# A running NaN-skipping row maximum: the last 36 tiles divided anew, single-buffer waits for the key passes, shared write-back semaphores from tile 42 on

## The chip, the cores and the metric

The kernel runs on one core of a Trainium2 chip. The metric is the time of one execution on the device in microseconds (us); lower is better. The profile was taken in one such execution.

## The reference

```python
def reference(x: np.ndarray, axis: int) -> np.ndarray:   # x: 32 x 2048 x 2048 f32, a tenth of it NaN; axis -1
    return np.nanmax(x, axis=axis).astype(np.float32)
```

Each of the 65,536 rows of 2048 numbers gives its largest number that is not a NaN. 536.87 MB are read and 0.26 MB written.

## The kernel before

Every one of the 128 partitions has 512 rows of x to itself. Work is counted in **quarters**: a quarter is 512 of a row's 2048 elements on all partitions, 256 KB in all, and there are 2048 of them. They are cut into 69 **tiles**, numbered from 0: tile 0 has 4 quarters, tiles 1 to 35 have 32 (8 rows), tiles 36 to 68 have 28 (7 rows). Three tiles fit into the buffer `full`.

A tile goes through four stages, one engine or queue each:

- **Load.** SP issues the DMA of a tile, in one or several pieces. The load of tile n waits for the last reduce of tile n-3, which frees the buffer (`free`, passed as `before`).
- **Key pass** (the ACTIVATE with `Prelu`, `e_key`). ScalarE (ACT) reads the upper 16 bits of each float and makes of it a number in which a NaN falls to the bottom. Below tile 38 (`PLAIN`) the keys are written over the upper half of the data itself; from there on into one of three **key buffers** (`kts`) of 12 quarters. One of these is a tile of its own, which the profile calls kt; the other two lie in a part of `full` that is free by then, so the profile calls them xt. When a chunk doesn't fit behind the last one, the next key buffer is taken, and the key pass has to wait until what was in it has been written back (`kfree`, `freed`).
- **Write-back** (`write`). The keys are turned back and put into the upper halves of the floats, with NaNs gone. GpSimd (POOL) does most, ACT some, and in tiles 1 to 33 VectorE (DVE) five quarters a tile.
- **Reduce** (`maxima`). DVE takes the maximum of a stretch of rows once its write-backs are there.

Which quarters go where is written out by hand in `TILES`, one entry a tile: the load pieces, then the chunks, each with its key passes and its write-backs, then the reduces, all in quarters. A plain number among the write-backs is POOL's. A pair (n, w) is ACT's and is issued after w more key passes; with w = -1 it is DVE's. Each engine runs its instructions in the order in which they are issued.

Two devices stand beside that table. `joints` looks for a reduce that needs exactly one last write-back of POOL and one of ACT; the two then raise one shared semaphore, `pairN_i`, in place of each engine's own, and whoever waits for one of the two waits for both. And `EARLY` is a list of tiles: in these, the last key pass of a tile, if it takes a new key buffer, waits for that buffer and for the one after it as well.

The lines that do this:

```python
kold = freed(key, (key + 1) % NKEYS) if number in EARLY and at + c == end else freed(key)
```

```python
pairs[number] = joints(keys, backs, reds)
```

Of the kernel before, what the change touches and what calls it, by code (L numbers as in the profile page):

```python
# [16 lines left out]
TILES = (  # L17
    [([4], [([4], [4])], [4])]
    + [([32], [([12], [(5, -1), 7]), ([12], [12]), ([8], [8])], [12, 12, 8])] * 32
# [14 lines left out]
    + [([28], [([7], [7]), ([9], [9]), ([12], [12])], [16, 12])] * 3  # L34
    + [([28], [([8], [1, (2, 2), 5]), ([6, 3], [9]), ([11], [11])], [16, 12])]
    + [([28], [([6], [6]), ([10], [10]), ([12], [12])], [16, 12])]
    + [([28], [([8], [8]), ([9], [9]), ([11], [11])], [8, 8, 12])] * 2
# [6 lines left out]
    + [([16, 12], [([8], [8]), ([8], [8]), ([12], [7, (5, 0)])], [8, 8, 12])] * 2  # L44
# [7 lines left out]
)  # L52


# [19 lines left out]
WIDE = 8  # L74
FULL = 36
PLAIN = 38

NARROW = (0, 17 * D // 2, 31 * D // 2)
BUFS = 3
# [7 lines left out]

LANES = 14

EARLY = (0, 1, 2, 3, 4, 5, 6, 7, 8, 9, 10, 11, 12, 13, 14, 15, 16, 17, 18, 19, 20, 21, 22, 23, 24, 25, 26, 27, 28, 29, 30, 31, 32, 33, 34, 35, 36, 37, 38, 39, 40, 41, 42, 43, 44, 45, 46, 47, 48, 49, 50, 51, 52, 53, 54, 55, 56, 63)  # L90

# [11 lines left out]
def joints(keys, backs, reds):  # L103


    parts = []
    pieces = []
    at = end = step = 0
    for n, wait in backs:
        end += n  # L110
        while at < end:
            at += keys[step]
            step += 1
        if wait is None or wait >= 0:
            parts.append((end - n, end, wait is not None, step + (wait or 0), len(pieces)))
        pieces.append(n)
    needs = []
    done = 0
    for n in map(abs, reds):
        over = [i for i, p in enumerate(parts) if p[0] < done + n and p[1] > done]  # L120
        done += n
        pools = [i for i in over if not parts[i][2]]
        acts = sorted((i for i in over if parts[i][2]), key=lambda i: parts[i][3])
        if pools and acts and parts[pools[-1]][3] > parts[acts[-1]][3]:
            acts = []
        needs.append(pools[-1:] + acts[-1:])
    pairs = {}
    for need in needs:
        if len(need) == 2 and all(sum(i in n for n in needs) == 1 for i in need):
            both = tuple(parts[i][4] for i in need)  # L130
            for i in both:
                pairs[i] = both
    return pairs
# [62 lines left out]
def kernel(  # L196
# [91 lines left out]
    with tc.tile_critical() as section:  # L288
# [72 lines left out]
        pairs = {}  # L361
        half = {}

        def write(number, a, b, k, kp, e, i, back):
# [27 lines left out]
            for a, b, k, back, when in both:  # L392
                if number >= PLAIN:
                    kfree[k][back] = max(kfree[k].get(back, ((0, 0), None)), (when, e))
                clean[number].append((a, b, e, back))

        def freed(*ks):

            uses = [(back, then, e) for k in ks for back, ((_, then), e) in kfree[k].items()]
            counts = [e[1] for _, _, e in uses if e[0] == "pool"]  # L400
            deps = []
            for back, then, e in uses:
                if back == "act" and order.count["act"] >= then:
                    e = ("act", then)
                if back != "pool" or e[0] == "pool" or all(v < then for v in counts):
                    deps.append(e)
            return deps
# [50 lines left out]
        for number, (loads, chunks, reds) in enumerate(TILES):  # L458
            keys = [k for ks, _ in chunks for k in ks]
            fresh = {}  # L460
            step = 0
            for ks, bs in chunks:
                assert number < PLAIN or sum(ks) * Q <= KEYS
                assert sum(ks) == sum(b[0] if isinstance(b, tuple) else b for b in bs)
                fresh[step] = sum(ks) * Q
                step += len(ks)
            backs = [b for _, bs in chunks for b in bs]
            backs = [b if isinstance(b, tuple) else (b, None) for b in backs]
            assert sum(loads) == sum(keys) == sum(b for b, _ in backs) == sum(map(abs, reds))
            pairs[number] = joints(keys, backs, reds)  # L470
            for i, part in enumerate(PARTS):
                if part[3] == number:
                    find_part(i)
# [3 lines left out]
            assert number < BUFS or state["tile"] > number - BUFS  # L477
            if number == PLAIN:
                for k in (1, 2):
# [23 lines left out]
            for step, c in enumerate(keys):  # L503
                c *= Q
                here = [l for a, b, l in landed if a < at + c and b > at]
                kold = []
                if number < PLAIN:
                    key = 0
                    kx = xt[:, at : at + c].bitcast(u16)[:, 1::2]
                elif used + fresh.get(step, 0) > KEYS:  # L510
# [3 lines left out]
                    assert all(q[2] != key for v in half.values() for q in v)  # L514
                    kold = freed(key, (key + 1) % NKEYS) if number in EARLY and at + c == end else freed(key)
                    kfree[key] = {}
                if number >= PLAIN:
                    kx = kts[key][:, used : used + c]
# [16 lines left out]
                while backs and lo + backs[0][0] * Q <= at:  # L535
# [3 lines left out]
                        kts[key][:, used - (at - lo) : used - (at - lo) + n]  # L539
                        if number >= PLAIN  # L540
                        else xt[:, lo : lo + n].bitcast(u16)[:, 1::2]
# [95 lines left out]
```

## Time and profile before

| what | value |
|---|---|
| time, median of 3 runs | 1258.86 us (1258.61 to 1261.85) |
| the profiled execution, its own time | 1259.93 us |
| its span, first to last instruction | 1258.1 us |
| busy: DVE, ACT, POOL | 1167.0 us (93%), 1142.9 us (91%), 1071.4 us (85%) |
| load and store queue | 537.14 MB, 99.1% of 16 engines' span |
| mean rate | 427 GB/s |

The profiled execution took 1.07 us longer than the median. The page's table of slices shows the busy share of each engine and the rate of the DMA in fortieths of the span; the chain of waits follows the work that ended last back to the start; a group of instructions has the mean time of one in ns, and the idle time of its engine ahead of it with what ended that. Instructions of one engine overlap by up to a tenth of a microsecond, so a group's mean is a little more than the distance between two starts.

### The profile page before, as it was taken

What the parts mean: (1) busy time and instruction counts of PE and PEld (TensorE: products, weight loads), DVE (VectorE), ACT (ScalarE), POOL (GpSimd) and SP (SyncE); (2) the same over time, 40 slices, a digit from 0 to 9 for tenths busy, and PEclk for the clock granted to TensorE, in tenths of its full rate; (3) what the DMA queues carried; (4) which work ended last, traced back from release to release, by engine and by line L of the source; (5) the groups of instructions that cost most, each with busy time, mean ns of one, the idle gap of its engine ahead of it and who ended that gap; (6) DMA issues with size and microseconds to landing.
All of it is one profiled execution on the core that took longest, in us unless ns stands there. A gap on an engine that the chain in (4) does not pass through costs nothing.

```text
span 1258.1 us, 1009 instructions
## 1 busy us (share of the span) xinstructions
DVE 1167.0 (93%) x245; ACT 1142.9 (91%) x287; POOL 1071.4 (85%) x249
## 2 busy tenths in 40 slices
DVE  0799999999999999999999997999887988999999
ACT  3999999999999999999999988898877779999997
POOL 0888788787988888989899997978998997999997
DMA  9999999999999999999999999999999999999996
GB/s 408 433 440 440 435 438 433 435 430 435 433 433 438 433 433 433 433 435 433 424 433 438 421 434 414 427 419 438 438 438 438 407 438 420 438 427 433 427 428 267
DMA packets 16664, 537.21 MB, mean 427 GB/s; under 512 B 2576, under 2 KB 2576, under 8 KB 5136
## 3 DMA queue, kind: packets, MB, share of 16 engines
q1 hardware_dynamic: 16656, 537.14, 99.1%
q14 instruction: 8, 0.07, 0.0%
HBM read 536.87 MB, written 0.26 MB: 427 GB/s over the span
## 4 chain that ended last, share of the span: by engine, by line
DMA 33%; DVE 28%; POOL 20%; ACT 19%; issue 1%; SPq 0%; DVEq 0%
DMA xt<-in_x_dram 33%; DVE acc L311 28%; POOL xt L304 20%; ACT xt L294 17%; ACT kt L294 2%; DVE xt L311 0%; SPq L281 0%; SPq L490 0%; DVE acc L318 0%; SPq L632 0%; DVEq L178 0%; SPq L288 0%
## 5 line engine op out<-in xcount | busy, mean ns | idle before, releaser
L311 DVE TENSOR_REDUCE acc<-xt 128x3 f32<-128x6144 f32 (+4 forms) x210 | 1112.3, 5347 | 69.8 <-POOL xt L304 64.4
L304 POOL TENSOR_SCALAR xt<-xt 128x4096 int16<-128x4096 uint16 (+9 forms) x201 | 921.0, 4582 | 156.2 <-ACT xt L294 145.4
L294 ACT ACTIVATE xt<-xt 128x6144 uint16<-128x6144 int16 (+14 forms) x224 | 960.7, 4382 | 74.0 <-DMA xt<-in_x_dram 73.5
L294 ACT ACTIVATE kt<-xt 128x6144 uint16<-128x6144 int16 (+10 forms) x41 | 140.9, 3452 | 31.1 <-POOL xt L304 30.9
L304 POOL TENSOR_SCALAR xt<-kt 128x6144 int16<-128x6144 uint16 (+10 forms) x33 | 145.3, 4403 | 21.2 <-ACT kt L294 19.2
L311 DVE TENSOR_SCALAR xt<-xt 128x2560 int16<-128x2560 uint16 x33 | 55.5, 1683 | 19.0 <-ACT xt L294 19.0
L294 ACT ACTIVATE xt<-kt 128x1536 int16<-128x1536 uint16 (+6 forms) x20 | 43.9, 2201 | 0.4
L326 POOL TENSOR_SCALAR late<-acc 128x112 int32<-128x112 f32 (+1 forms) x5 | 2.8, 559 | 0.4
L294 ACT ACT_TABLE_LOAD x1 | 1.3, 1283 | 1.3 <-SPq L288 1.3
L340 POOL TENSOR_TENSOR acc<-acc,late 128x112 int32<-128x112 int32 (+1 forms) x5 | 2.0, 398 | 0.4
L311 DVE TENSOR_REDUCE xt<-xt 128x1 f32<-128x1536 f32 x1 | 1.7, 1743 | 0.0
L346 POOL MEMSET scalars<- 128x1 f32 x1 | 0.1, 99 | 0.9 <-SPq L288 0.9
L618 POOL MEMSET const-float32-0.0<- 128x1 f32 x1 | 0.1, 99 | 0.2 <-issue 0.2
L294 ACT ACTIVATE scalars<-scalars 128x1 f32<-128x1 f32 x1 | 0.2, 203 | 0.0
L318 DVE SCALAR_TENSOR_TENSOR acc<-acc 128x7 f32<-128x7 f32 x1 | 0.2, 167 | 0.0
L618 POOL MEMSET const-uint8-127<- 128x1 uint8 x1 | 0.1, 103 | 0.0
L618 POOL MEMSET const-bfloat16-1.0<- 128x1 bf16 x1 | 0.1, 102 | 0.0
L618 POOL MEMSET const-float32-1.0<- 128x1 f32 x1 | 0.1, 99 | 0.0
## 6 DMA issues: line engine op xcount, KB each, us to landing
xt<-in_x_dram SPq DMA_DIRECT2D x22, 7168.0 KB, 22.2
xt<-in_x_dram SPq DMA_DIRECT2D x3, 3584.0 KB, 24.8
xt<-in_x_dram SPq DMA_DIRECT2D x3, 3072.0 KB, 21.9
xt<-in_x_dram SPq DMA_DIRECT2D x2, 4096.0 KB, 15.9
xt<-in_x_dram SPq DMA_DIRECT2D x6, 1280.0 KB, 23.6
xt<-in_x_dram SPq DMA_DIRECT2D x1, 6400.0 KB, 20.8
xt<-in_x_dram SPq DMA_DIRECT2D x2, 2816.0 KB, 20.5
xt<-in_x_dram SPq DMA_DIRECT2D x3, 1792.0 KB, 24.6
```

The lines of the kernel that those rows point to most:

```text
L294: lambda: nc.scalar.activation(**kw),
L304: lambda: nc.gpsimd.tensor_scalar(**kw),
L311: return order.add("dve", nc.vector, lambda: do(**kw), deps)
L318: lambda: engine.scalar_tensor_tensor(out=acc, in0=acc, scalar=0.0, in1=acc, op0=ALU.mult, op1=ALU.add),
L326: lambda: engine.tensor_scalar(out=none, in0=acc, scalar1=LEAST, scalar2=float(0x00400000), op0=ALU.is_lt, op1=ALU.mult,),
L340: lambda: engine.tensor_tensor(out=bits, in0=bits, in1=none, op=ALU.add),
L346: e_top = order.add("pool", nc.gpsimd, lambda: nc.gpsimd.memset(top, EDGE), [])
L618: nc = _bacc.Bacc("TRN2", target_bir_lowering=False, num_devices=1)
```

## The change

Three things change. The entries of `TILES` from tile 33 on are other ones: still 36 tiles of the same sizes, cut differently into loads (114 in place of 110 in the whole kernel), key passes (248, before 246), write-backs (POOL 238 of 1755 quarters, before 234 of 1767; ACT 44 of 133, before 39 of 116; DVE 32 of 160, before 33 of 165) and reduces (219, before 211). `EARLY` is empty, so that each key pass waits for its own key buffer alone. And `joints` is asked only from tile 42 on (`PAIRED`).

```diff
+    + [([30, 2], [([12], [12]), ([12, 8], [12, 6, (2, 2)])], [12, 12, 8])]                      # tile 33
-    + [([18, 14], [([12], [(5, -1), 7]), ([6], [6]), ([6], [6]), ([8], [8])], [12, 12, 8])]
...
+    + [([28], [([4], [(4, 2)]), ([6], [6]), ([6], [6]), ([4, 8], [4, 8])], [4, 12, 4, 8])]      # tile 39
-    + [([28], [([4], [(4, 2)]), ([9, 3], [8, 4]), ([12], [12])], [16, 12])]
...
+    + [([28], [([8], [(2, 1), 6]), ([8], [8]), ([12], [(3, 1), 9])], [16, 12])]                 # tile 55
+    + [([24, 4], [([10], [10]), ([9], [(4, 0), 5]), ([9], [(3, 0), 6])], [16, 12])]             # tile 56
-    + [([28], [([8], [(1, 1), 7]), ([8], [8]), ([12], [(5, 0), 7])], [16, 12])]
-    + [([28], [([9], [9]), ([10], [10]), ([9], [7, (2, 0)])], [8, 8, 12])]
...
+PAIRED = 42
...
-EARLY = (0, 1, 2, 3, 4, 5, 6, 7, 8, 9, 10, 11, 12, 13, 14, 15, 16, 17, 18, 19, 20, 21, 22, 23, 24, 25, 26, 27, 28, 29, 30, 31, 32, 33, 34, 35, 36, 37, 38, 39, 40, 41, 42, 43, 44, 45, 46, 47, 48, 49, 50, 51, 52, 53, 54, 55, 56, 63)
+EARLY = ()
...
-            pairs[number] = joints(keys, backs, reds)
+            pairs[number] = joints(keys, backs, reds) if number >= PAIRED else {}
```

What that does to the order is shown at three places. The rows are one engine's instructions in the order of issue, with the semaphores that each waits for: `order_load` is a load's landing, `order_pool`, `order_act` and `order_dve` are an engine's own count. 512 elements are one quarter.

ACT in tile 39, before. An ACTIVATE from int16 data into a key buffer is a key pass; the 128x2048 that waits for `order_act` is ACT's own write-back of four quarters:

```order
L294 ACTIVATE xt<-xt 128x2048 [waits order_act,order_load0]
L294 ACTIVATE xt<-xt 128x4608 [waits order_pool]
L294 ACTIVATE xt<-xt 128x1536
L294 ACTIVATE xt<-xt 128x2048 [waits order_act]
L294 ACTIVATE kt<-xt 128x6144 [waits order_pair39_2]
```

ACT in tile 39, after:

```order
L299 ACTIVATE xt<-xt 128x2048 [waits order_act,order_pool,order_load0]
L299 ACTIVATE xt<-xt 128x3072
L299 ACTIVATE xt<-xt 128x3072 [waits order_pool]
L299 ACTIVATE xt<-xt 128x2048 [waits order_act]
L299 ACTIVATE kt<-xt 128x2048 [waits order_pool]
L299 ACTIVATE kt<-xt 128x4096
```

The last twelve quarters are two key passes now, and the first of these waits for POOL's count alone, at an older write-back, where one key pass waited for a pair of this same tile.

ACT in tiles 55 and 56, before, from the second key pass of tile 55 to the end of the passes and write-backs of tile 56:

```order
L294 ACTIVATE xt<-xt 128x4096 [waits order_pair54_2]
L294 ACTIVATE xt<-xt 128x512 [waits order_act]
L294 ACTIVATE kt<-xt 128x6144 [waits order_pair55_2]
L294 ACTIVATE xt<-kt 128x2560 [waits order_act]
L294 ACTIVATE xt<-xt 128x4608 [waits order_load3]
L294 ACTIVATE xt<-xt 128x5120
L294 ACTIVATE kt<-xt 128x4608 [waits order_pool]
L294 ACTIVATE xt<-kt 128x1024 [waits order_act]
```

The same after:

```order
L299 ACTIVATE xt<-xt 128x4096 [waits order_pair54_2]
L299 ACTIVATE xt<-kt 128x1024 [waits order_act]
L299 ACTIVATE xt<-xt 128x6144 [waits order_pair54_3]
L299 ACTIVATE kt<-xt 128x5120 [waits order_act,order_pool,order_load4]
L299 ACTIVATE xt<-xt 128x1536
L299 ACTIVATE xt<-xt 128x4608 [waits order_pair55_2]
L299 ACTIVATE xt<-xt 128x2048 [waits order_act]
L299 ACTIVATE xt<-xt 128x4608 [waits order_pair55_4,order_load5]
L299 ACTIVATE xt<-xt 128x1536 [waits order_act]
```

The twelve-quarter key pass of tile 55 waited for a pair of tile 55; now it waits for one of tile 54, and the pairs of tile 55 are waited for by key passes of tile 56.

DVE in tiles 32 to 34, before and after, is the third place. A TENSOR_SCALAR is DVE's write-back of five quarters:

```order
L311 TENSOR_SCALAR xt<-xt 128x2560 [waits order_act]
L311 TENSOR_REDUCE acc<-xt 128x3 [waits order_dve,order_pool]
L311 TENSOR_REDUCE acc<-xt 128x3 [waits order_pool]
L311 TENSOR_REDUCE acc<-xt 128x2 [waits order_pool]
L311 TENSOR_REDUCE acc<-xt 128x3 [waits order_pool] x2
```

```order
L316 TENSOR_REDUCE acc<-xt 128x3 [waits order_pool] x2
L316 TENSOR_REDUCE acc<-xt 128x2 [waits order_act,order_pool]
L316 TENSOR_REDUCE acc<-xt 128x3 [waits order_pool] x2
L316 TENSOR_REDUCE acc<-xt 128x2 [waits order_pool]
L316 TENSOR_REDUCE acc<-xt 128x3 [waits order_act,order_pool] x2
```

DVE has no write-back in tile 33 any more, and a reduce that needs ACT and POOL below tile 42 waits for two counts.

More of the change, by code (lines that the diff above doesn't have):

```diff
@@ L19 @@
     + [([32], [([12], [(5, -1), 7]), ([12], [12]), ([8], [8])], [12, 12, 8])] * 32
[10 rows of a table removed]
[10 rows of a table added]
     + [([28], [([9], [9]), ([12], [12]), ([7], [(7, 0)])], [8, 20])]
     + [([28], [([9], [9]), ([12], [3, 9]), ([7], [(7, 0)])], [12, 16])]
[2 rows of a table removed]
[L34 to L37, printed above, removed]
[6 rows of a table removed]
-    + [([16, 12], [([8], [8]), ([8], [8]), ([12], [7, (5, 0)])], [8, 8, 12])] * 2
[5 rows of a table removed]
[22 rows of a table added]
     + [([5, 3, 5, 3, 4, 3, 3, 2], [([4, 4, 4], [(2, 1), 2, 4, 3, (1, 1)]), ([4], [4]), ([4, 3, 3, 2], [(1, 1), 3, 3, (1, 1), 4])], [4, 4, 4, 4, 4, 4, 4])]
[1 row of a table removed]
[1 row of a table added]
 )
```

49 rows, old and new, of the table TILES are left out of this document.

## The prediction

> **What bounds the kernel now.** I read the page first, then the chain of waits, the waits by engine, the instructions in order of time at four places, and the groups by shape. From the page:
>
> ```profile
> DVE 1167.0 (93%) x245; ACT 1142.9 (91%) x287; POOL 1071.4 (85%) x249
> q1 hardware_dynamic: 16656, 537.14, 99.1%
> ```
>
> The load queue is nearly always busy, so only two things can shorten the run: loads that land closer together, and less work between the last landing and the end. The chain of waits shows both (start, length, what):
>
> ```profile
> 599.19 25.24 DMA xt<-in_x_dram
> ...
> 729.19 22.60 DMA xt<-in_x_dram
> ...
> 762.57 2.47 POOL xt L304
> ...
> 765.07 5.33 ACT kt L294
> ...
> 770.47 7.05 POOL xt L304
> 777.55 6.57 DVE acc L311
> 784.13 19.33 DMA xt<-in_x_dram
> ...
> 848.28 23.09 DMA xt<-in_x_dram
> ...
> 916.40 22.64 DMA xt<-in_x_dram
> ...
> 1003.81 22.12 DMA xt<-in_x_dram
> ...
> 1062.48 193.21 DVE acc L311 x54
> ```
>
> A DMA piece runs from a load's issue to its landing: 729.19 + 22.60 = 751.79 is the landing of tile 39, the others are tiles 42 (803.46), 46 (871.37), 50 (939.04) and 55 (1025.93). From 46 to 50 four loads land in 67.67 us, 16.92 us each, the pace of a full queue. Against it, 39 to 42 lost 51.67 - 3 x 16.92 = **0.9 us** and 50 to 55 lost 86.89 - 5 x 16.92 = **2.3 us**; 42 to 46 lost 0.2. Tile 42's load shows why: at the pace the load ahead of it lands at 751.79 + 33.84 = 785.6, and it is issued only 1.5 us before that, since DVE frees the buffer at 784.1. Landing 19.33 us after issue, it found an empty queue. Its wait is the chain POOL, ACT, POOL, DVE ahead of it, each engine idle while the other works.
>
> From 1062.48 on, DVE has no gap until the end. DVE's lateness at that moment is carried to the end, less what DVE gains on the loads.
>
> **The mechanism that makes DVE late.** In order of time, with the idle time ahead of an instruction and what ended it in brackets:
>
> ```profile
> 765.07 5.32 ACT L294 ACTIVATE kt<-xt 128x6144 uint16<-128x6144 int16 x1 [3.65 <-POOL xt L304]
> 770.47 7.04 POOL L304 TENSOR_SCALAR xt<-kt 128x6144 int16<-128x6144 uint16 x1 [5.44 <-ACT kt L294]
> ...
> 952.12 4.90 ACT L294 ACTIVATE kt<-xt 128x5632 uint16<-128x5632 int16 x1 [4.19 <-POOL xt L304]
> 957.10 6.48 POOL L304 TENSOR_SCALAR xt<-kt 128x5632 int16<-128x5632 uint16 x1 [5.01 <-ACT kt L294]
> 988.47 0.33 SPq L490 DMA_DIRECT2D xt<-in_x_dram  x1
> ...
> 1038.71 5.32 ACT L294 ACTIVATE kt<-xt 128x6144 uint16<-128x6144 int16 x1 [4.97 <-POOL xt L304]
> 1044.12 4.20 POOL L304 TENSOR_SCALAR xt<-kt 128x3584 int16<-128x3584 uint16 x1 [5.44 <-ACT kt L294]
> ```
>
> Three times (tiles 39, 50, 55) the last key pass of a tile waits for the write-back that POOL has just begun, and POOL then has nothing to do for 5.0 to 5.4 us while that key pass runs. By `EARLY` the pass waits for the next key buffer too, which holds the first chunk of this same tile; a shared semaphore makes that wait reach to a POOL write-back of the second chunk. All such waits between 733 and 1063 us:
>
> ```profile
> ACT kt L294 <- POOL xt L304: 30.9, 16, 5.0
> ACT xt L294 <- DMA xt<-in_x_dram: 25.7, 11, 4.1
> POOL xt L304 <- ACT kt L294: 18.6, 6, 5.4
> ```
>
> The change takes this wait away: a key pass then waits only for write-backs of three chunks back, some 17 us old, and the rows of the order at tiles 39 and 55 show it.
>
> **The change part by part.** Durations come from the groups by shape (count, busy, mean ns of one):
>
> ```profile
> L304 POOL TENSOR_SCALAR xt<-kt 128x6144 int16<-128x6144 uint16 x7 | 49.3, 7047 | 6.5 <-ACT kt L294 6.1
> L304 POOL TENSOR_SCALAR xt<-kt 128x4096 int16<-128x4096 uint16 x4 | 19.1, 4769 | 1.6 <-ACT kt L294 1.3
> L304 POOL TENSOR_SCALAR xt<-kt 128x3072 int16<-128x3072 uint16 x1 | 3.6, 3629 | 0.1
> L294 ACT ACTIVATE kt<-xt 128x6144 uint16<-128x6144 int16 x12 | 63.8, 5319 | 13.7 <-POOL xt L304 13.6
> L294 ACT ACTIVATE kt<-xt 128x4096 uint16<-128x4096 int16 x2 | 7.2, 3618 | 1.7 <-POOL xt L304 1.7
> L294 ACT ACTIVATE xt<-kt 128x2048 int16<-128x2048 uint16 x2 | 5.0, 2483 | 0.0
> L311 DVE TENSOR_REDUCE acc<-xt 128x3 f32<-128x6144 f32 x93 | 609.0, 6552 | 33.1 <-POOL xt L304 29.7
> L311 DVE TENSOR_REDUCE acc<-xt 128x2 f32<-128x4096 f32 x71 | 312.2, 4415 | 5.3 <-POOL xt L304 5.2
> ```
>
> Per quarter, a key pass is 0.45 us, a write-back 0.59 to 0.62 on either engine, a reduce 0.55. Numbers of quarters between are taken in proportion.
>
> *Tile 39 and the loss at tile 42.* Data lands at 751.8. Keys of 4, 6 and 6 quarters end at 759.1 (16 x 0.455), ACT's write-back of 4 at 761.6, keys of 4 and 8 at 767.0. POOL starts its first 6 at 756.5, after the second key pass and after tile 38; 6 and 6 end at 763.8, 4 at 766.4, 8 at 771.9 (begun at 767.1). DVE's three rows run from 763.8 to 770.4, one row to 772.6, two rows to 777.0. Before, it was 784.1. The load of tile 42 then leads by 8.5 us instead of 1.5: **0.9 us of supply** won.
>
> *Tiles 47 to 56 and the loss at tile 54.* Here POOL has 250 quarters in place of 264, ACT 30 write-back quarters in place of 16. A tile wholly on POOL costs it 28 x 0.587 = 16.4 us and some 0.25 between instructions, against 16.92 of supply; a gap of 5.0 us, as at 957.10, is not made up, and 31 us later the load of tile 54 is issued at 988.47, about 2 us ahead of the landing before it (939.04 + 3 x 16.92 = 989.8). 14 quarters less are 8.2 us off POOL over ten tiles, and the gap itself goes. ACT pays 14 x 0.6 = 8.4 us, covered by its 25.7 us of waiting for landings. Without that cover it would cost up to 0.8 us a tile. I count **2.3 us of supply**.
>
> *Tiles 55, 56 and the end.* Tile 55 lands at 1025.9. Keys of 8, 8, ACT's write-back of 2, key of 12: 1029.5, 1033.1, 1034.5, 1039.8. POOL's 6 end at 1033.2, its 8 at 1038.1, its 9 at 1045.2. DVE's four rows go from 1038.1 to 1046.8, and the three rows, which wait for ACT's 3 quarters behind the next key pass, from 1047 to 1053.6. Tile 56's load of 24 quarters lands at 1040.4 (16.92 x 24/28 after tile 55). Its keys and write-backs: 10 end on ACT at 1044.9, 3 of tile 55 at 1046.8, 9 at 1050.9, 4 at 1053.4, 9 at 1057.4; on POOL 10 end at 1051.1, 5 at 1054.3, 6 at 1061.0. DVE's four rows end at 1063.0, its three at 1069.5. Before, three rows and two rows were left from 1062.48: 1062.48 + 4.4 + 6.5 = 1073.4. So DVE is **3.9 us** earlier against the same landings. The same sum for tile 58 leaves 3.4 us. How much reaches the end is read there:
>
> ```profile
> 1244.58 11.09 DVE L311 TENSOR_REDUCE acc<-xt 128x1 f32<-128x2048 f32 x5
> ...
> 1247.53 8.70 SPq L586 DMA_DIRECT2D out_dram<-acc  x3
> 1248.57 1.33 POOL L304 TENSOR_SCALAR xt<-kt 128x1024 int16<-128x1024 uint16 x1 [0.28 <-ACT kt L294]
> ```
>
> The first store waits for the last landing, so that was at 1247.53. The last write-backs are done at 1249.90; DVE ends at 1255.67 and began its last row 2.31 us before, at 1253.36. So no more than **3.46 us** can be won here, whatever DVE's lead; then the key passes and write-backs of the last quarters set the end. From tile 57 on, the numbers of reduces (52) and rows are as before. I take **3.1 us**, from 0 to 3.46.
>
> *Tiles 33 to 38.* DVE loses a write-back of five quarters, 1.7 us, and gains one reduce; POOL has 144 quarters for 145 in four more instructions (0.25 each); ACT gets 8 write-back quarters in place of 2, 4 us more:
>
> ```profile
> 640.00:660.00 20.00, 19.73 (x4) 20.00 (x5) 19.68 (x5) 1.00 1.01 434
> 660.00:680.00 20.00, 19.90 (x5) 20.00 (x6) 19.68 (x5) 1.00 0.98 425
> 740.00:760.00 20.00, 16.87 (x5) 17.93 (x7) 17.13 (x4) 1.00 1.02 442
> ```
>
> DVE, ACT and POOL (columns two to four) are full there. POOL comes last in each tile; my sum has it end tile 36 where it did, with ACT 3.5 us later but still ahead of it. I count nothing, with 4 us of loss or 1.7 us of gain (DVE's write-back, and the chain's 1.7 us of lost supply from tile 32's landing, 624.43, to 751.79: 208 quarters at 16.92/28 are 125.7 of 127.4 us) as ends.
>
> *Waits.* Reduces below tile 42 and key passes now wait for up to three counts. The trace has no such row alone; the nearest is the 0.02 to 0.08 us of issue between two links of the chain. Two a tile are at most 0.2 us against 1.8 us that DVE has over (16.92 less 15.1): nothing.
>
> **The sum.** 1259.93 - 0.9 - 2.3 - 3.1 = 1253.6 us for an execution like the profiled one; the median of the runs lies 1.07 us lower: **1252.6 us**.
>
> **The rivals.** *Only one of the two pays* (the end stays tied to DVE, or the loads slip elsewhere): 1258.86 - 3.2 = 1255.7. The three sums lean on means, and each tile in between could bring a wait. *Waits only change their name*: key passes wait for their own buffer as long as they did for the next one, and nothing moves: 1258.9. The order speaks against it, since POOL's writes three chunks back end before the tile lands. *More than I count*: tiles 33 to 38 give back their 1.7 us and the end its full 3.46: 1250.5.
>
> *Slower: ACT in tiles 33 to 38.* If its 4.2 us more come through to POOL and aren't made up, DVE ends tile 56 at 30.5 + 4.2 us behind the landing; beyond 3 x 16.92 - 19.33 = 31.4 each load waits for its buffer, and the end is 4.2 us later: 1263.1. It decides as soon as ACT, not POOL, ends last in tiles 36 to 38. For it: ACT is at 20.00 of 20. Against it: the 25.7 us of waits for landings that follow, and 17.93 of 20 by 740.
>
> *Slower: four more loads.* A DMA with hardly any data takes 1.4 us to land:
>
> ```profile
> out_dram<-acc SPq DMA_DIRECT2D x1, 3.5 KB, 1.4
> 1235.00:1240.00 5.00, 5.00 (x3) 5.00 (x7) 4.75 (x3) 1.00 1.03 419
> ```
>
> Were each new load to stand alone, 4 x 1.4 = 5.6 us would be lost and no gain got: 1264.5. But where the small loads of the last tiles follow each other, the DMA share stays at 1.03 and the rate at 419 GB/s. The Trainium skill, in DMA: Bandwidth & Descriptors, section Rules for kernel authors, asks for at least 1 MiB in a DMA for the most bandwidth, and three of the four tiles that gain a load get a piece below it or at it. By that rule the change would lose; the trace agrees only in the step from 434 to 419 GB/s, under 0.1 us a megabyte.
>
> **How the numbers follow.** Both gains 0.56; more than I count 0.08; one of two 0.16; same waits 0.06; ACT 0.12; loads 0.02. A measurement of this kernel can tell about 0.3%, 3.8 us, from no change: 1255.1 and 1262.6. One of two lies at that edge and is split in half, so faster is 0.56 + 0.08 + 0.08 = 0.72, same 0.08 + 0.06 = 0.14, slower 0.14. The first three cases hold 0.80: from 1250.5 less a microsecond of spread, 1249.5, up to 1258.0.
>
> **What would show it.** Right: no idle time over 2 us of POOL ahead of a write-back from kt after 733 us; tile 42's load issued near 777; 16.9 us a load from 751 to 1060; the last landing near 1244.3, DVE's end 5 us behind it, the last reduces waiting or nearly so. Wrong: ACT full beyond 740 us with POOL waiting for it; a new landing interval above 17.5 us; DVE still 8 us behind the last landing.

## The result, and the profile after

The changed kernel takes 1252.04 us (1252.01 to 1252.12, median of 4 runs) against 1258.73 us (1258.56 to 1261.85) for the kernel before: a ratio of 0.9941, 95% interval 0.9924 to 0.9958. The profiled execution took 1252.06 us and its span is 1250.3 us, where the one before had 1259.93 and 1258.1.

The page after, the rows that answer to those of before:

```profile
DVE 1164.8 (93%) x252; ACT 1151.3 (92%) x294; POOL 1060.2 (85%) x253
q1 hardware_dynamic: 17232, 537.14, 99.5%
```

ACT is busy 8.4 us longer, as the table asks, and the queue is a little fuller. POOL's 11.2 us less say little: the table takes 12 quarters off POOL, some 7 us, and e7 below, with the same table, has POOL busy for 1070.4 us. The chain of waits after (start, length, what):

```profile
624.44 82.36 ACT xt L299 x20
...
742.69 25.31 DMA xt<-in_x_dram
...
812.23 23.33 DMA xt<-in_x_dram
...
862.25 24.03 DMA xt<-in_x_dram
...
914.04 22.95 DMA xt<-in_x_dram
...
981.05 23.64 DMA xt<-in_x_dram
...
1032.08 23.38 DMA xt<-in_x_dram
...
1166.85 80.96 DVE acc L316 x31
1247.83 0.17 DVE acc L323
```

Start plus length of a DMA piece is a landing: tile 40 at 768.00, tile 44 at 835.56, 47 at 886.28, 50 at 936.99, 54 at 1004.69, 57 at 1055.46. From the first to the last that is 17 loads in 287.46 us, 16.91 each, with no slower stretch among them. The last piece of the chain, DVE alone, which began at 1062.48, begins at 1166.85.

The waits by engine from 733 to 1063 us (what was waited for: total, times, longest), after:

```profile
DVE acc L316 <- POOL xt L309: 28.9, 21, 2.9
ACT kt L299 <- DMA xt<-in_x_dram: 27.9, 11, 5.0
POOL xt L309 <- ACT xt L299: 24.5, 13, 5.4
POOL xt L309 <- ACT kt L299: 16.7, 9, 4.4
ACT xt L299 <- DMA xt<-in_x_dram: 13.9, 7, 4.3
```

The row of ACT waiting for POOL (30.9 us before, 16 times) is gone: whenever ACT waits here, it waits for data. POOL waits for ACT as long as before, 41.2 us in two rows instead of 40.9, so what went is the wait in one direction alone, and POOL's idle time as such did not have to shrink. At the three places of the prediction, and at the end, in order of time after:

```profile
766.08 4.75 POOL L309 TENSOR_SCALAR xt<-kt 128x4096 int16<-128x4096 uint16 x1 [0.41 <-ACT kt L299]
776.25 0.33 SPq L495 DMA_DIRECT2D xt<-in_x_dram  x1
783.48 5.33 POOL L309 TENSOR_SCALAR xt<-kt 128x4608 int16<-128x4608 uint16 x1 [4.38 <-ACT kt L299]
...
1035.22 5.34 POOL L309 TENSOR_SCALAR xt<-xt 128x4608 int16<-128x4608 uint16 x1 [1.44 <-ACT xt L299]
...
1241.13 6.67 DVE L316 TENSOR_REDUCE acc<-xt 128x1 f32<-128x2048 f32 x3
1243.18 5.17 SPq L591 DMA_DIRECT2D out_dram<-acc  x3
1244.06 1.33 POOL L309 TENSOR_SCALAR xt<-kt 128x1024 int16<-128x1024 uint16 x1 [0.15 <-ACT kt L299]
```

Tile 42's load is issued at 776.25 instead of 784.13. The last data land at 1243.18, and DVE is done at 1247.80, 4.6 us behind them instead of 8.1. The last write-back ends at 1245.39 and DVE's last row began 2.31 us before its end, at 1245.49: DVE still has no gap there, but its backlog is down to 0.1 us. An earlier DVE alone would win no more than that, since its last row needs the key and write-back of the last quarters.

### The profile page after: what moved, and what is told of

The parts are those of the page before. It is cut to its first block, busy times and chain, and to the rows that moved or that the text cites. A ratio compares the mean times of both kernels' runs of the same rounds, so it can differ in the third digit from the quotient of the medians.

```text
span 1250.3 us, 1057 instructions
## 1 busy us (share of the span) xinstructions
DVE 1164.8 (93%) x252; ACT 1151.3 (92%) x294; POOL 1060.2 (85%) x253
## 4 chain that ended last, share of the span: by engine, by line
DMA 38%; DVE 25%; ACT 23%; POOL 14%; issue 1%; SPq 0%; ACTq 0%
DMA xt<-in_x_dram 38%; DVE acc L316 24%; ACT xt L299 21%; POOL xt L309 14%; ACT kt L299 2%; SPq L495 0%; SPq L286 0%; DVE acc L323 0%; SPq L637 0%; ACTq L183 0%; SPq L293 0%
## 5 line engine op out<-in xcount | busy, mean ns | idle before, releaser
L316 DVE TENSOR_REDUCE acc<-xt 128x3 f32<-128x6144 f32 (+3 forms) x219 | 1114.6, 5135 | 64.2 <-POOL xt L309 56.7
L309 POOL TENSOR_SCALAR xt<-xt 128x3584 int16<-128x3584 uint16 (+9 forms) x204 | 926.3, 4541 | 162.8 <-ACT xt L299 152.9
L299 ACT ACTIVATE xt<-xt 128x6144 uint16<-128x6144 int16 (+12 forms) x236 | 1006.3, 4361 | 62.8 <-DMA xt<-in_x_dram 61.9
L309 POOL TENSOR_SCALAR xt<-kt 128x4096 int16<-128x4096 uint16 (+10 forms) x34 | 128.8, 3789 | 21.2 <-ACT kt L299 19.7
L299 ACT ACTIVATE kt<-xt 128x4096 uint16<-128x4096 int16 (+10 forms) x42 | 118.9, 2852 | 29.7 <-DMA xt<-in_x_dram 29.4
L316 DVE TENSOR_SCALAR xt<-xt 128x2560 int16<-128x2560 uint16 x32 | 52.6, 1644 | 19.0 <-ACT xt L299 19.0
L299 ACT ACTIVATE xt<-kt 128x1536 int16<-128x1536 uint16 (+6 forms) x14 | 29.6, 2112 | 0.2
```

The costliest lines, as they stand in the source:

```text
L299: lambda: nc.scalar.activation(**kw),
L309: lambda: nc.gpsimd.tensor_scalar(**kw),
L316: return order.add("dve", nc.vector, lambda: do(**kw), deps)
```

## The experiments

The theory was that one thing pays, the wait of a last key pass, through `EARLY` and a shared semaphore, on a write-back of its own tile. Its rivals: the new division of the tiles pays (14 quarters less on POOL in tiles 47 to 56), or the smaller number of shared semaphores does. Beside each group of runs the kernel before was run again: its median is 1259.09 us for e1 to e4, 1258.93 for e5 to e8 and 1258.78 for e10 and e11, and ratios and gains go by that.

**e1_own_buffer_only**: the kernel before, its table and its shared semaphores kept.

```diff
-EARLY = (0, 1, 2, ..., 56, 63)
+EARLY = ()
```

> Kernel before with EARLY empty, nothing else. Theory W (the wait of a tile's last key pass for the next key buffer makes DVE late; the new table is the smaller part): the waits in tiles 39, 50 and 55 go, the load of tile 42 leads by about 5 us, loads land 16.9 us apart, DVE ends tile 56 some 4 us earlier: 1252.5 to 1254. Theory T (the new table does it, by taking 14 quarters off POOL in tiles 47 to 56; the waits are hidden in time that POOL has anyway): 1257.5 to 1258.7.

Measured 1251.95 us (1251.85 to 1253.57), ratio 0.9943 (0.9928 to 0.9958): the whole gain with none of the new table. Its waits from 733 to 1063 us have no row of ACT behind POOL, and its end looks like that of after:

```profile
ACT xt L294 <- DMA xt<-in_x_dram: 52.1, 18, 4.6
...
POOL xt L304 <- ACT kt L294: 8.0, 6, 2.8
```

```profile
1242.92 5.22 SPq L586 DMA_DIRECT2D out_dram<-acc  x3
...
1247.62 0.17 DVE L318 SCALAR_TENSOR_TENSOR acc<-acc 128x7 f32<-128x7 f32 x1
```

**e2_pairs_from_42**: the kernel before with the new rule for shared semaphores alone, `EARLY` kept.

```diff
-            pairs[number] = joints(keys, backs, reds)
+            pairs[number] = joints(keys, backs, reds) if number >= 42 else {}
```

> Kernel before with shared semaphores only from tile 42 on, EARLY as before. Theory W: only the wait of tile 39 goes (its pair is off), those of tiles 50 and 55 stay: the 0.9 us of supply at tile 42 are won and nothing else, 1257.6 to 1258. Theory T: 1258.7.

Measured 1257.86 us (1257.36 to 1259.68), ratio 0.9991 (0.9981 to 1.0): about 1 us, as far as it can be told from nothing. It removes the stall of tile 39 and leaves those of tiles 50 and 55, where POOL still has 5.01 and 5.44 us of idle time ahead of the write-back. Its waits of ACT for POOL from 733 to 1063 us:

```profile
ACT kt L294 <- POOL xt L304: 26.3, 15, 5.0
```

**e3_three_pairs_off**: the kernel before, `EARLY` and table kept, without shared semaphores in three tiles.

```diff
-            pairs[number] = joints(keys, backs, reds)
+            pairs[number] = {} if number in (39, 50, 55) else joints(keys, backs, reds)
```

> Kernel before without shared semaphores in tiles 39, 50 and 55 alone; EARLY and the table as before. Theory W: in these three tiles the last key pass no longer waits for the second chunk's write-back, and the result is within 1 us of the kernel with EARLY empty: 1252.5 to 1254. Theory T: 1258 to 1258.7. A third one (EARLY's waits in all tiles cost a little each): little more than 1 us of gain here, and all of it with EARLY empty.

Measured 1251.98 us (1251.82 to 1252.07), ratio 0.994 (0.9926 to 0.9955). ACT still waits for the second buffer, but now for a write-back that is old; the 30.9 us of that wait became

```profile
ACT kt L294 <- POOL xt L304: 7.8, 12, 1.7
```

The three long waits were 12.8 us of the 30.9; the others shrank with them. So it is the two devices together that made the stall, and either can be taken away. The shared semaphores of three tiles (one each in tiles 39 and 50, two in tile 55) hold the whole gain.

**e4_new_table_only**: the kernel after, with `EARLY` and all shared semaphores as they were before.

```diff
-PAIRED = 42
+PAIRED = 0
...
-EARLY = ()
+EARLY = (0, 1, 2, ..., 56, 63)
```

> Kernel after with EARLY and shared semaphores in all tiles as in the kernel before: the new table alone. Theory W: waits for pairs of the same tile come back where the new table has them (tile 55: the 12-quarter key pass waits for pair55_2, about 3.5 us), loads mostly at pace, DVE later at the end: 1253.5 to 1256. Theory T: 1252 to 1252.5.

Measured 1257.49 us (1256.79 to 1258.52), ratio 0.9986 (0.9977 to 0.9996). The new table alone is worth 0.14%, and stalls of this kind turn up in its order too: in tile 55 through a shared semaphore as before, and in tile 49 through `EARLY` alone, where the last key pass waits for POOL's write-back of the tile's first chunk of twelve quarters. In order of time, tile 49 first:

```profile
932.91 7.99 ACT L299 ACTIVATE xt<-xt 128x5120 uint16<-128x5120 int16 x2 [4.78 <-POOL xt L309]
...
1035.16 5.32 ACT L299 ACTIVATE xt<-xt 128x6144 uint16<-128x6144 int16 x1 [3.82 <-POOL xt L309]
...
1040.57 5.34 POOL L309 TENSOR_SCALAR xt<-xt 128x4608 int16<-128x4608 uint16 x1 [5.44 <-ACT xt L299]
```

The last row is the write-back of tile 55 that the table after has at 1035.22 with 1.44 us ahead of it. Beside e1, which has the old table, the kernel after gains nothing from the new one: 1252.04 and 1251.95.

**e5_pair50_off** and **e6_pair55_off**: the kernel before without the shared semaphores of one tile only, to see which stall pays where.

```diff
-            pairs[number] = joints(keys, backs, reds)
+            pairs[number] = {} if number == 50 else joints(keys, backs, reds)
```

and the same with 55.

> Kernel before without the shared semaphore in tile 50 alone. The prediction's split into supply and end: only the late loads of tiles 52 to 54 are won (2.3 us), DVE is as late behind the landing at tile 56 as before (30.5 us) and ends 8 us behind the last landing: about 1256.4. If the two terms were one (any of the three waits makes DVE late for good): 1252 to 1254, or no change.

> Kernel before without the shared semaphore in tile 55 alone. By the split: loads land as before, DVE ends tile 56 some 26.5 us behind its landing and ends about 4.7 us behind the last landing in place of 8.2: 1255.3. If the two terms were one: 1252 to 1254, or no change.

Measured 1257.27 us (1256.87 to 1258.34), ratio 0.9987 (0.9978 to 0.9996), and 1255.68 us (1255.01 to 1257.15), ratio 0.9974 (0.9965 to 0.9983). In order of time, first e5, then e6:

```profile
952.02 6.48 POOL L304 TENSOR_SCALAR xt<-kt 128x5632 int16<-128x5632 uint16 x1 [0.83 <-ACT kt L294]
...
1041.18 4.19 POOL L304 TENSOR_SCALAR xt<-kt 128x3584 int16<-128x3584 uint16 x1 [5.44 <-ACT kt L294]
...
1244.58 8.69 SPq L586 DMA_DIRECT2D out_dram<-acc  x3
```

```profile
956.76 6.48 POOL L304 TENSOR_SCALAR xt<-kt 128x5632 int16<-128x5632 uint16 x1 [5.01 <-ACT kt L294]
...
1038.68 4.19 POOL L304 TENSOR_SCALAR xt<-kt 128x3584 int16<-128x3584 uint16 x1 [0.66 <-ACT kt L294]
...
1246.40 5.06 SPq L586 DMA_DIRECT2D out_dram<-acc  x3
```

and the end of both chains, in the same order:

```profile
1252.74 0.17 DVE acc L318
```

```profile
1250.94 0.17 DVE acc L318
```

The two stalls do different things. Without that of tile 50 the last data land at 1244.58, but DVE still ends 8.1 us behind them: supply (data that land earlier) is won, the end is not. Without that of tile 55 they land at 1246.40 and DVE ends 4.5 us behind: the end is won. DVE's lateness at tile 56 says the same: it ends that tile 30.5 us behind its landing in e5, as before, and 26.7 us in e6. I had put e5 at 1256.4 and e6 at 1255.3; both gained less, by 0.9 and 0.4 us. The three single removals (e2, e5, e6) sum to 6.1 us (1.23 + 1.66 + 3.25) of 7.1 in e3. The runs of each of the three spread over more than the 1.0 us that is left, so whether a part comes only when all go is not shown.

**e7_pairs_everywhere**: the kernel after with shared semaphores in all tiles again.

```diff
-PAIRED = 42
+PAIRED = 0
```

> Kernel after with shared semaphores in all tiles (PAIRED at 0); EARLY empty, the new table. Theory W: without EARLY no key pass waits for a young pair, so that the switch from tile 42 on is worth nothing: 1251.9 to 1252.3. If shared semaphores hurt below tile 42 by themselves: 1253 or more.

Measured 1252.09 us (1252.06 to 1252.12), ratio 0.9944 (0.9931 to 0.9958). With `EARLY` empty, the shared semaphores below tile 42 cost nothing.

**e8_fewer_loads**: e1 with fewer and larger loads in the last three tiles.

```diff
-[5, 7, 5, 6, 5]
+[12, 11, 5]
-[5, 3, 5, 3, 4, 3, 3, 2]
+[8, 8, 7, 5]
-[3, 2, 3, 2, 2, 1, 1, 3, 2, 2, 1, 2, 2, 1, 1]
+[5, 5, 4, 5, 3, 2, 2, 1, 1]
```

> The kernel with EARLY empty and the old table, in which the loads of tiles 66, 67 and 68 are cut into 3, 4 and 9 pieces in place of 5, 8 and 15. The landings of these tiles lie 17.1, 17.2 and 17.5 us apart where tiles with one piece take 16.9, about 0.037 us a piece: 12 pieces fewer make the last landing 0.4 us earlier, and the time 0.3 to 0.45 us shorter than with EARLY empty alone (1251.95), if no reduce then waits for a landing. If a piece costs 1.4 us (the rival of the prediction, a load that stands alone): up to 16 us shorter. If pieces cost nothing, or DVE then waits: 1252 or more.

A miss: 1255.1 us (1254.57 to 1255.96), ratio 0.9969 (0.9957 to 0.998), 3 us slower than e1. DVE in this kernel, in order of time from 1100 us to the last reduce:

```profile
1096.07 106.38 DVE L311 TENSOR_REDUCE acc<-xt 128x2 f32<-128x4096 f32 x25
1203.91 2.29 DVE L311 TENSOR_REDUCE acc<-xt 128x1 f32<-128x2048 f32 x1 [1.45 <-POOL xt L304]
1206.47 2.29 DVE L311 TENSOR_REDUCE acc<-xt 128x1 f32<-128x2048 f32 x1 [0.27 <-POOL xt L304]
1209.24 41.96 DVE L311 TENSOR_REDUCE acc<-xt 128x1 f32<-128x2048 f32 x19 [0.48 <-ACT xt L294]
```

In e1 the same stretch is one row:

```profile
1099.38 148.20 DVE L311 TENSOR_REDUCE acc<-xt 128x2 f32<-128x4096 f32 x45
```

and DVE has no gap from there to the end. Here its run breaks off at 1202.45, and it stands idle for 2.2 us ahead of the next three rows, most of the 3 us. Those rows are of tile 66: its first piece, now of twelve quarters, lands at 1199.38, where the first piece of five quarters in e1 lands at 1194.17. The third row needs an ACT write-back that is issued behind a key pass of the second piece, and that piece lands at 1206.04. Small pieces are there for an early start; twelve fewer of them brought the landings of these three tiles only 0.3 us closer together (51.5 us in place of 51.8).

**e10_split_loads**: e1 with seventeen loads cut in four, to price a piece.

```diff
 tiles 40 to 56, each:
-[28]
+[7, 7, 7, 7]
```

> The kernel before with EARLY empty (the kernel of e1_own_buffer_only), and the loads of tiles 40 to 56 cut into four pieces of 7 quarters (1.8 MB) where they were one piece of 28 (7.3 MB): 51 more loads, nothing else. It prices a load piece. Theory: pieces that follow each other in the queue cost about 0.04 us each, so the last landing is 1.9 us later and the time is 1252 to 1254 us. Rival (the prediction's, a piece costs 1.4 us): the seventeen tiles land 21 us apart and the time is over 1310 us. A third way: shorter pieces let the key passes of a tile begin earlier, which changes nothing here, since DVE is not late for lack of keys; then 1251.9.

Measured 1254.35 us (1254.22 to 1254.88), ratio 0.9964 (0.995 to 0.9978): 2.4 us more than e1 for 51 pieces, just above the expected range. The windows of e1 and of this kernel (start and end; the stretch; DVE, ACT, POOL; clock; DMA share; GB/s), and its DMA issues:

```profile
768.00:900.00 132.00, 118.65 (x18) 119.64 (x32) 111.94 (x25) 1.00 1.00 435
```

```profile
768.00:900.00 132.00, 122.44 (x18) 120.23 (x33) 116.14 (x25) 1.00 1.01 431
```

```profile
xt<-in_x_dram SPq DMA_DIRECT2D x28, 1792.0 KB, 23.0
```

From 435 to 431 GB/s: 0.05 us a piece (2.5 us by the landings of tiles 39 to 56, divided by 51). For pieces that queue behind each other, the 1.4 us of the prediction's rival is out by a factor of nearly thirty. The Trainium skill, in DMA: Bandwidth & Descriptors, section Rules for kernel authors, asks for at least 1 MiB in a DMA; by that rule pieces of 7168 and of 1792 KB are both large enough and there is nothing to lose, where these runs show a small loss. For smaller pieces the nearest run is e8, where twelve fewer of 0.25 to 1.75 MB each won 0.3 us.

**e11_no_shared_semaphores**: the kernel after without any.

```diff
-PAIRED = 42
+PAIRED = 69
```

> The kernel after with no shared write-back semaphores at all (PAIRED = 69). Theory: once a key pass waits for its own buffer alone, a shared semaphore holds nothing up and saves nothing that can be measured: 1252.0 to 1252.3 us, DVE's end 4.6 us behind the last landing. Rival: waiting for two counts in place of one costs a reduce some tenths of a microsecond, 27 tiles of it, mostly where DVE has no slack (from tile 57 on): 1253 us or more.

A miss, small and outside the spread: 1252.67 us (1252.65 to 1252.75), ratio 0.995 (0.9935 to 0.9965). DVE's end is 4.4 us behind the last landing, so it is not DVE that pays. The last loads are issued as in after, and land 0.9 us later; first after, then this kernel:

```profile
1196.25 36.48 SPq L495 DMA_DIRECT2D xt<-in_x_dram  x17
```

```profile
1196.22 36.48 SPq L495 DMA_DIRECT2D xt<-in_x_dram  x17
...
1244.08 0.40 SPq L591 DMA_DIRECT2D out_dram<-acc  x1
```

The stores begin at 1243.18 in the one and at 1244.08 in the other. What holds the data up is open (last section).

## Why the prediction was right, and where its steps were off

The forecast was 1252.6 us, and the mechanism is the one it names. By its steps, on the two profiled executions (7.87 us apart, 6.3 forecast):

- **Tile 39 and tile 42's load**: 0.9 forecast. The load is issued at 776.25 (forecast 777), and tiles 39 to 42 land in 50.66 us instead of 51.67: 1.0 us. Right.
- **Tiles 47 to 56**: 2.3 forecast. Tiles 50 to 55 land in 84.60 us instead of 86.89: 2.3 us. The size was right, half of the reason was not. I put 8.2 us of POOL's relief beside the vanished gap; e1 and e3, with the old 264 quarters on POOL, have the whole gain. The gap alone was the cause.
- **The end**: 3.1 forecast out of at most 3.46. Measured 3.5, the whole of it: the bound read from the rows of before was exact. DVE ends tile 56 26.36 us behind its landing instead of 30.54, a lead of 4.2 us (3.9 forecast), enough to reach the bound. I should have taken the bound.
- **Tiles 33 to 38**: nothing forecast, between 4 us of loss and 1.7 of gain. Measured 0.7 of gain: tile 32 to tile 39 land in 126.7 us instead of 127.4. That is not the change's: it is one load, tile 38, which took 18.57 us in the profiled execution of before, while the one slow load of this stretch takes 17.87 to 17.94 in all other profiles, those with the old table too (last section). My counts of quarters there were those of tiles 33 to 37; with tile 38 POOL writes back 167 for 169 in seven more instructions and ACT 13 for 6. ACT did become the engine of the chain, 82.36 us from 624.44 on, and was at its full 20.00 of 20 up to 740 us, as a window of after shows (start and end; the stretch; DVE, ACT, POOL); from 740 to 760 it has 19.12 of 20. That was for the slower rival; what it needed beside, POOL and DVE late through ACT, did not come: DVE ends tile 38 at 759.4 us, where e1 with the old table ends it at 762.5.

```profile
720.00:740.00 20.00, 20.00 (x8) 20.00 (x7) 19.32 (x8) 1.00 0.96 416
```

- **Tiles 42 to 46**: left out of the sum. They give 0.3 us (67.57 us instead of 67.91).
- **The median.** I took 1.07 us off, because the profiled execution of before was that much longer than the median. Some 0.7 of it is probably the slow load of tile 38; the runs that make the median have no profile. The medians are 6.7 us apart where the sum has 6.3. The three terms as measured, 1.0, 2.3 and 3.5, make 6.8, which fits: what was missing is the end, taken 0.4 too small.

Of the signs, two were badly chosen. One said that the prediction is right: POOL does idle more than 2 us ahead of a write-back from kt, 4.38 us at 783.48. This is no stall of the old kind: ACT was not waiting for POOL then, as the waits show, but still making keys. The sign should have been the row ACT behind POOL, which is what went. The other said that it is wrong: a new landing interval above 17.5 us. After has one of 17.89, at tile 39, but it is the slow load that before had at tile 38, and no buffer was late for it.

The other cases are told apart by the runs. "Waits only change their name" is what the new table does with the old waits (e4), and not what the change does. "Only one of two" is what e5 and e6 do, each with its own half. The rival of the four loads is out: 51 more cost 2.4 us. Where I was lucky is the table: I counted it as half a cause, and it is worth nothing once the waits are gone.

## What to carry to other kernels

When an engine waits with its partner idle in the next row, ask which instruction the wait is really for: a semaphore that two engines share makes everyone who waits for one wait for both, and three such waits were worth 0.6% here. A stall that delays the release of a buffer until the queue runs dry costs supply, one from which the last engine is busy without a gap costs the end, and each has its own bound in the profile of before. Before dividing work anew, take the wait away by itself: it may be all there is.

## What was not expected of the hardware

In each of the twelve profiles, one load between 716 and 768 us lands about 1 us late (1.7 in the profiled execution of before), though it was issued 3.2 to 5.9 us ahead of the landing before it: in e1, tile 38 lands 17.88 us after tile 37, and the loads around it come 16.9 us apart; in after it is tile 39, with 17.89. In eleven of the twelve, a packet of 8 KB of the instruction queue falls into just that load; in e2 it falls 30 us later. On the page, the DMA queues of after and of e11 read

```profile
q14 instruction: 8, 0.07, 0.0%
```

```profile
q14 instruction: 9, 0.07, 0.0%
```

and the ninth packet of e11 comes at 1240.1 us, in the load that was 0.9 us late. But other such packets (in after at 914.3 and 954.5 us) stand in loads that are on time, and in e1 one at 1236.4 us stands in the last load, which is not late; and the slow load of e2 has none. So the packet is not enough by itself, and the cause of both delays is open; no run was made to settle it.

A piece of a load that queues behind another costs about 0.05 us, not the 1.4 us that a small DMA takes by itself.
